# Encoder step: the last quarter of gate a moved from plain gate products into seven-product units; loads, output rows and the last product in another order

## The chip, the cores and the metric

The kernel runs on one core of a Trainium2 chip, in one launch. The metric is the device time of the whole program in microseconds (us). TensorE (PE) multiplies, VectorE (DVE) and ScalarE (ACT) do elementwise work, GpSimd (POOL) a little of it; SyncE (SP), POOL and ACT issue DMAs.

## The reference

One inference step of a one-layer encoder over 1024 prompt rows and 64 sample rows, 1088 in all, model width 1024:

```python
proj = rmsnorm(x, g_mix) @ w_in                     # 1024 -> 5120
cb, cc, ch, q, k, v, ga, gb = split(proj)           # six of 512, then ga and gb of 1024
ya = (cb * conv3(cc * ch)) @ w_conv_out             # 512 -> 1024, causal, width 3
yb = band_attention(q, k, v, rel_bias) @ w_attn_out # 8 heads of 64, own chunk of 64 and 8 before it
x  = x + (sigmoid(ga) * ya + sigmoid(gb) * yb) @ w_out
x  = x + (silu(n @ w_ff1) * (n @ w_ff3)) @ w_ff2    # n = rmsnorm(x, g_ffn)
y  = rmsnorm(x, g_final)
```

Outputs are also the last conv rows and the newest keys and values. All is float32.

## The kernel before

*Precision.* Each operand is split into a rounded high part and a low part (`split`, L128 on ACT and L129 on DVE), and a product is three matmuls: high by high, high by low, low by high. Activations lie transposed, with 1088 tokens in two halves of 544 columns (HT), each made of two pieces of 272 (HN).

*Units of seven.* A projection of 256 output channels can run as a unit (`run`, L277): the 2x2 blocks of weights and of tokens are combined so that seven block products do the work of eight (`STEPS`), each of 4 blocks x 3 x 2 pieces. The sums of the operands lie in `xn` and `xs`. q, k, cc, ch, cb and three quarters of gate a (`ga` 0 to 2) are such units, then four units `ya` of half the depth, whose operands `uforms` writes over those of the projections during the last unit before them. Results of ga get a sigmoid and go to `ga_d` in DRAM; `gated_load` fetches them, `ya_done` multiplies (the last quarter of ya is stored without its gate), and the rows go to `y_d`. One quarter of `xn`, which ya overwrites in part, is kept in `x21_d` and reloaded on SP before the gates.

*Gates and attention.* The other gate channels are plain products (`gate`, L343 to L345), with eight matmuls where a unit has seven: the eight blocks of gate b, then blocks 6 and 7 of gate a. A gate has four pieces of 272 columns, 24 matmuls each. Attention is a generator of 75 steps, nine token tiles for each of eight heads: scores, softmax, transposition two steps later, product with the values three steps later. After each gate piece `between` runs PER = 3.15 steps, so gate matmuls fill the time in which PE would wait for a softmax. The first eight pieces have no steps: they cover the loads of head 0 (`head_load`). Before the last LAST = 2 gates the remaining steps are flushed; the two gates after that cover the way of the head rows: `combine` stores them in `o_d`, they are loaded into `ob`, scaled by the softmax sums (L1160) and split. The last two gates write their sigmoids to SBUF (`ga_rows`).

*Output rows.* For each of eight blocks m, `yb` (L343 to L345 again, on `ob`) is multiplied by sigmoid(gb) (L1187), added to the row of y (L1188) and split into `mg`; the 64 sample columns are split once more into `ms`. For m of 6 and 7 the row of y is first multiplied by `ga_rows` (L1179). `rows_in` loads the rows four blocks ahead. Then come the product with w_out in two halves of columns (`wo_half`, loaded on SP), the feed-forward units (tiles `Aa` to `Db`), and the down product (L1750), whose last tiles pass the final norm (`half_ended`) to the output.

*Order.* The Tile scheduler orders each engine's instructions when it builds the program: by the order of the program text and by its own estimate of when operands are ready, so that a later instruction can be put ahead of one that it expects to wait. `tc.issue_after(i)` adds an edge behind instruction i on the same engine. On the chip each engine then runs its list in order.

Of the kernel before, what the change touches and what calls it, by code (L numbers as in the profile page):

```python
# [66 lines left out]
def encoder_kernel(ctx: ExitStack, tc: tile.TileContext, ins, outs):  # L67
# [268 lines left out]
    def product(out, w, x, o, n):  # L336

        kt = 4 * len(w)
        for k in range(kt):
            a, b = (t[:, k % 4] for t in w[k // 4])  # L340
            p, q = x.at(0, k, o, n), x.at(1, k, o, n)
            first, then = (q, p) if x is xn and o // HN % 2 == 0 else (p, q)
            mm(out, a, first, start=k == 0, stop=False)  # L343
            mm(out, a, then, start=False, stop=False)  # L344
            mm(out, b, p, start=False, stop=k == kt - 1)  # L345

    PIECES = [(j * HN, HN) for j in range(4)]
    GATES = [("b", m) for m in range(8)] + [("a", m) for m in range(6, 8)]
    for g, m in GATES:
# [3 lines left out]
        plan.append((ld, KD, m % 2 * P))  # L353
    for m in range(0, 8, 2):
        ld = {"src": ins["w_attn_out"][0][:, m * P : (m + 2) * P], "w": 2 * P, "at": 40}
        plan += [(ld, 4, j * P) for j in range(2)]
# [353 lines left out]
    def ya_done(u):  # L710
        def f(r, h, src, snap):
            if u == 3:
                s = summed(src, snap, "ya")
            else:
                g = gated.pop((u, r, h))
                if snap is None:
                    s = snap1(None, "ya")
                    two = [t.rearrange("p (j n) -> p j n", j=2) for t in (s, g)]
                    vec.tensor_tensor(two[0], src, two[1], op=ALU.mult)
                else:  # L720
                    s = summed(src, snap)
                    vec.tensor_tensor(s, s, g, op=ALU.mult)
            nc.gpsimd.dma_start(row_of(y_d, u, r, h), s)

        return f
# [110 lines left out]
    for n in range(len(units)):  # L836
        if n in (5, 6):
            for j in range(2):
                table_store(2 * (n - 5) + j)
        if n in (4, 5):  # L840
            for j in range(2):
                table_load(2 * (n - 4) + j, slot(STAGE, 768))
        if n == 0:
            r, si = r0, 2
        else:
            if n + 1 < len(units):
                nxt_unit = unit_of(n + 1)
                new = [(nxt_unit, {1: (), 2: (0, 1, 2)} if n == 1 else {})]
            else:
                new = [(PlainNext(), {})]  # L850
            if n == 1:
                ahead += new
                r, si = r1, 2
            else:
                r, si = run1(n, unit, new), 0
            unit = nxt_unit
        if n >= 12 and n < 15:
            gated_load(n - 12)
        if n == 14:
            plain_load(0)  # L860
        for _ in r:
            if n == 12:
                uforms(si)
            if n < 2 and si in (2 + n, 5 + n):
                i = 2 * n + si // 5
                cache_tile(i)
                if i + 2 < 4:
                    cache_load(i + 2)
            if si > 1:
                for f in due:  # L870
                    f()
                due.clear()
            due += late
            late.clear()
            si += 1
# [37 lines left out]
    sm2 = at_pool.tile([P, 2, 9], F32, name="sm2", bufs=1)  # L913
    nc.gpsimd.memset(sm2, 1.0)

    def head_load(h):
# [9 lines left out]
        for l in range(2):  # L926
# [7 lines left out]
        nc.sync.dma_start(v.bitcast(F32), v_d[h, :TP].rearrange("(b p) e -> p b e", p=P))  # L934
# [3 lines left out]
        b = bb[:, h % 2]  # L938
        near = bias_d[h, 127 : 127 + P * 383].rearrange("(p n) -> p n", n=383)
        far = bias_rows(h, 0, 384)  # L940
        nc.sync.dma_start(b[:HD, :384], far[:HD])
        nc.sync.dma_start(b[HD:, HD:384], far[HD:, HD:])
        nc.sync.dma_start(b[:HD, 384:576], near[:HD, :192])
        nc.sync.dma_start(b[HD:, 384:], near[HD:, :256])
        heads[h] = (q, k, ks, v, vs, b)

# [176 lines left out]
    def rows_in(m):  # L1123
        t, z = rows[m] = u_rows.tile([P, T], F32, tag="yg", name=f"yg{m}"), row_tile((m % 5 + 1) % 2, f"gb{m}")
        nc.sync.dma_start(z, gb_d[m * P : (m + 1) * P])
# [3 lines left out]

    for l in range(2):  # L1130
        nc.sync.dma_start(xn.t[0, 1][:, :, l].bitcast(F32), x21_d[:, l])
    for i in range(4):
# [8 lines left out]
    for i in range(4, len(GATES)):  # L1141
        gate_w[i] = next_w()
        if i == len(GATES) - LAST:
# [7 lines left out]
            u_rows = pg_stack.enter_context(tc.tile_pool(name="u_rows", bufs=5, reuse_waits="tile"))  # L1151
            ga_rows = [uo.tile([P, T], F32, name=f"ga{m}") for m in (6, 7)]
            for k in range(2):
                split(ob.t[:, 0, k], ob.t[:, 1, k], o_rows[k])
            late_r = row_tile(1, "rc2"), row_tile(0, "rc3")
            for k, r in zip((2, 3), late_r):
# [4 lines left out]
                split(ob.t[:, 0, k], ob.t[:, 1, k], r)  # L1161
            for m in range(4):
                rows_in(m)
# [8 lines left out]
    for m in range(8):  # L1172
        wb = next_w()
        if m + 4 < 8:
            rows_in(m + 4)
        t, z = rows.pop(m)
        act.activation(z, z, AF.Sigmoid)
        if m >= 6:
            vec.tensor_tensor(t, t, ga_rows[m - 6], op=ALU.mult)  # L1179
# [27 lines left out]
    def wo_half(hf):  # L1207
        r = []
        for kq in range(2):
            raw = rpool.tile([P, 4, 512], F32, tag="raw", name=f"wor{hf}_{kq}")  # L1210
            nc.sync.dma_start(
                raw,
# [471 lines left out]

    def half_ended(i, d):


        x = acc[i, d]
        ssq = dp.tile([P, 1], F32, tag=f"ssq{d}", name=f"ssq{i}_{d}", bufs=2)
        act.activation(ring_of(1)[:, 3072:3584], x, AF.Square, accum_out=ssq)  # L1690
        if i not in parts:
# [12 lines left out]
    for b, ks in enumerate(blocks):  # L1704
        first, final = b == 0, b == len(blocks) - 1
        nk = blocks[b + 1] if not final else []
        for g in range(2):
# [28 lines left out]
            for si, js in turns:  # L1736
                p, ht = STEPS[si], hts[base + si]
                key = {1: "A", 6: "A", 5: "A", 3: "A", 2: "B", 7: "D", 4: "D"}[p]
                for j in js:
# [6 lines left out]
                    t = ps[key, j]  # L1746
                    for k, kp in enumerate(ks):
                        w = W2[kp].w[p]
                        for n, (x, l) in enumerate(((0, 0), (0, 1), (1, 0))):
                            mm(  # L1750
                                t, ht[k][:, j, x], w[:, l],
                                start=p in (1, 2, 7) and k == 0 and n == 0,
                                stop=k == len(ks) - 1 and n == 2, skip_group_check=p in (6, 5, 4, 3),
                            )
# [4 lines left out]
                    if first and fresh:  # L1759
                        sums_at[0] = act.copy(o, t).ins  # L1760
# [7 lines left out]
                    if final and p in (5, 4, 3):  # L1768
                        half_ended(i + 4 * h, d)
                if js[-1] == 0:  # L1770
# [66 lines left out]
```

## Time and profile before

| what | us |
|---|---|
| median of 3 runs (1464.16 to 1465.11) | 1465.03 |
| the profiled execution | 1465.99 |
| its span, first to last instruction | 1464.2 |
| PE busy in the span | 1447.3 |
| DVE busy | 996.1 |
| ACT busy | 681.6 |
| POOL busy | 144.5 |

Matmuls overlap in the pipeline, so that the sum of their durations says little; a stretch divided by its count of matmuls gives the pace. A wait in square brackets is the idle time of the engine before an instruction, with what ended it. Names are those of the program's tiles.

### The profile page before, as it was taken

What the parts mean: (1) busy time and instruction counts of PE and PEld (TensorE: products, weight loads), DVE (VectorE), ACT (ScalarE), POOL (GpSimd) and SP (SyncE); (2) the same over time, 40 slices, a digit from 0 to 9 for tenths busy, and PEclk for the clock granted to TensorE, in tenths of its full rate; (3) what the DMA queues carried; (4) which work ended last, traced back from release to release, by engine and by line L of the source; (5) the groups of instructions that cost most, each with busy time, mean ns of one, the idle gap of its engine ahead of it and who ended that gap; (6) DMA issues with size and microseconds to landing.
All of it is one profiled execution on the core that took longest, in us unless ns stands there. A gap on an engine that the chain in (4) does not pass through costs nothing.

```text
span 1464.2 us, 26244 instructions
## 1 busy us (share of the span) xinstructions
PE 1447.3 (99%) x10128; PEld 1359.8 (93%) x10128; DVE 996.1 (68%) x1845; ACT 681.6 (47%) x1368; POOL 144.5 (10%) x262
## 2 busy tenths in 40 slices
PE   8999999999999999999999999999999999999997
PEld 6899999999999989998889999999999999888886
DVE  7975475658357677583588667766666668857676
ACT  7654343336357666541455444444344445512223
POOL 1400010001211121000100111111011111000000
PEclk9999999999999999999999999999999999999999
DMA  8686522234787675834432444443334448877685
GB/s 287 183 277 224 177 75 72 67 111 167 254 233 210 175 196 140 290 122 135 158 109 78 162 160 158 151 168 126 123 132 169 148 180 312 281 229 250 208 269 202
DMA packets 157212, 262.47 MB, mean 179 GB/s; under 512 B 18496, under 2 KB 89344, under 8 KB 157088
## 3 DMA queue, kind: packets, MB, share of 16 engines
q1 hardware_dynamic: 134416, 188.53, 40.7%
q0 software_dynamic: 21520, 70.19, 13.4%
q8 instruction: 79, 1.29, 0.4%
q10 hardware_dynamic: 1152, 2.10, 0.4%
q14 instruction: 45, 0.37, 0.1%
HBM read 171.78 MB, written 90.81 MB: 179 GB/s over the span
## 4 chain that ended last, share of the span: by engine, by line
PE 75%; issue 14%; DVE 5%; DMA 3%; ACT 2%; POOL 1%; SPq 0%; POOLq 0%; ACTq 0%; DVEq 0%
PE Ab L277 9%; PE Aa L277 8%; PE A L1750 8%; PE Db L277 4%; PE Da L277 4%; PE D L1750 4%; PE B L1750 2%; PE Bb L277 2%; PE Ba L277 2%; PE wo L1229 2%; PE wo L1231 2%; PE wo L1230 2%; PE t L1040 2%; PE Ak L277 2%; PE Aq L277 2%
## 5 line engine op out<-in xcount | busy, mean ns | idle before, releaser
L343 PE MATMUL g<-xn,wp 128*128 128x272 f32 x320 | 94.0, 294 | 0.0
L344 PE MATMUL g<-xn,wp 128*128 128x272 f32 x320 | 93.2, 291 | 0.0
L345 PE MATMUL g<-xn,low 128*128 128x272 f32 x320 | 92.9, 290 | 0.0
L128 ACT CAST ring<-w2r 128x512 fp32r<-128x512 f32 (+1 forms) x78 | 42.8, 587 | 94.9 <-PE A L1750 50.2
L951 DVE CUSTOM_DVE_ANT_0 p<-s,bb 128x640 f32<-128x640 f32 (+5 forms) x72 | 47.6, 663 | 39.8 <-DMA gb_d<-gst 27.2
L1750 PE MATMUL A<-ring,low 128*128 128x512 f32 x264 | 72.4, 389 | 0.0
L1750 PE MATMUL A<-ring,ht 128*128 128x512 f32 x264 | 72.3, 390 | 0.0
L129 DVE TENSOR_TENSOR low<-rawa,wa 128x512 fp32r<-128x512 f32 x55 | 37.7, 687 | 42.0 <-ACT wa L128 42.0
L343 PEld LDWEIGHTS g<-xn,wp 128*128 128x128 f32 x320 | 60.3, 189 | 0.6
L344 PEld LDWEIGHTS g<-xn,wp 128*128 128x128 f32 x320 | 60.3, 188 | 0.6
L345 PEld LDWEIGHTS g<-xn,low 128*128 128x128 f32 x320 | 60.2, 188 | 0.4
L1750 PEld LDWEIGHTS A<-ring,low 128*128 128x128 f32 x264 | 49.6, 188 | 10.3
L1750 PEld LDWEIGHTS A<-ring,ht 128*128 128x128 f32 x264 | 49.3, 188 | 10.5 <-ACT acc L1760 0.4
L129 DVE TENSOR_TENSOR ring<-w2r,ring 128x512 fp32r<-128x512 f32 (+1 forms) x78 | 48.9, 647 | 14.3 <-ACT ring L128 14.1
L277 PE MATMUL Ab<-tt,wb 128*128 128x272 f32 x352 | 57.8, 285 | 0.4 <-ACT wb L128 0.4
L277 PE MATMUL Ab<-mg,wb 128*128 128x272 f32 x352 | 58.0, 286 | 0.0
L277 PE MATMUL Aa<-mg,wa 128*128 128x272 f32 x352 | 57.7, 285 | 0.0
L277 PE MATMUL Aa<-tt,wa 128*128 128x272 f32 x352 | 57.7, 285 | 0.0
L961 ACT ACTIVATE p<-p,mx 128x640 f32<-128x640 f32 (+5 forms) x72 | 50.8, 706 | 13.5 <-DVE mx L951 13.2
L128 ACT CAST wa<-rawa 128x512 fp32r<-128x512 f32 x55 | 34.0, 621 | 47.1 <-PE Ab L277 33.3
L129 DVE TENSOR_TENSOR pt<-t,pt 128x640 fp32r<-128x640 f32 (+2 forms) x64 | 41.8, 653 | 15.5 <-ACT pt L128 14.7
L128 ACT CAST wb<-rawb 128x512 fp32r<-128x512 f32 x55 | 34.0, 621 | 38.3 <-PE Aa L277 24.5
(583 smaller groups left out, 4504.0 us busy)
## 6 DMA issues: line engine op xcount, KB each, us to landing
h_d<-hq POOLq DMA_DIRECT2D x44, 512.0 KB, 4.2
ht<-h_d SPq DMA_DIRECT2D x77, 256.0 KB, 3.5
low<-h_d SPq DMA_DIRECT2D x77, 256.0 KB, 3.8
h_d<-hq_early POOLq DMA_DIRECT2D x29, 512.0 KB, 4.0
rawa<-in_w_ff SPq DMA_DIRECT2D x11, 1024.0 KB, 5.7
rawb<-in_w_ff SPq DMA_DIRECT2D x11, 1024.0 KB, 5.4
w2r<-in_w_ff SPq DMA_DIRECT2D x11, 1024.0 KB, 7.3
qd<-q_d SPq DMA_DIRECT2D x32, 272.0 KB, 4.1
```

Source lines behind the costliest of these rows:

```text
L128: a = act.copy(hi, src)
L129: b = vec.tensor_tensor(lo, src, hi.bitcast(F32), op=ALU.subtract)
L277: newest[0] = mm(t[:, j, :HN], w[:, k, :], x[p][:, k, l, j * HN : (j + 1) * HN], start=p in (1, 2, 7) and k == 0 and n == 0, stop=k == las ...
L343: mm(out, a, first, start=k == 0, stop=False)
L344: mm(out, a, then, start=False, stop=False)
L345: mm(out, b, p, start=False, stop=k == kt - 1)
L951: vec.tensor_tensor_reduce(out=s if len(ps.shape) == 2 else s.rearrange("p (a b) -> p a b", a=2), in0=ps, in1=bias if len(ps.shape) == 2 e ...
L961: act.activation(s, s, AF.Exp, bias=mx, scale=-1.0, accum_out=sm)
L1040: nc.tensor.transpose(tp[:, i * P : (i + 1) * P], s[:, i * P : (i + 1) * P], ident)
L1229: mm(ps, x(k, 0), wh, start=f, stop=False)
L1230: mm(ps, x(k, 1), wh, start=False, stop=False)
L1750: mm(t, ht[k][:, j, x], w[:, l], start=p in (1, 2, 7) and k == 0 and n == 0, stop=k == len(ks) - 1 and n == 2, skip_group_check=p in (6, 5 ...
```

## The change

- Gate a's last quarter becomes a unit `ga` 3 in front of the ya units. `GATES` keeps the eight blocks of b; LAST is 1, PER is 3.8. `uforms` and the gate loads move on by one unit, and all four quarters of ya are multiplied by their gate in `ya_done`. `ga_rows` and its products disappear.
- The reload of `x21_d` is cut in two: blocks 2 and 3 during the first ya unit, 0 and 1 at the old place.
- For head 0 the four bias loads are issued ahead of the three value loads.
- The first block's yb products are ordered behind the last gate's last matmul.
- The sample columns are split by two POOL operations for each m, instead of two each on ACT and DVE.
- w_out is loaded by POOL's queue instead of SP's.
- The very last down product runs as two halves of 256 columns, with its addition and sum of squares in halves too.

```diff
-PER = 3.15
-LAST = 2
+PER = 3.8
+LAST = 1
...
-    GATES = [("b", m) for m in range(8)] + [("a", m) for m in range(6, 8)]
+    GATES = [("b", m) for m in range(8)]
...
-        ("ga", 1), ("cb", 1), ("ga", 2),
+        ("ga", 1), ("cb", 1), ("ga", 2), ("ga", 3),
...
     def ya_done(u):
         def f(r, h, src, snap):
-            if u == 3:
-                s = summed(src, snap, "ya")
-            else:
-                g = gated.pop((u, r, h))
...
+            g = gated.pop((u, r, h))
...
+    def x21_load(k):
+        for l in range(2):
+            nc.sync.dma_start(xn.t[0, 1][:, k : k + 2, l].bitcast(F32), x21_d[:, l, k : k + 2])
...
-        if n >= 12 and n < 15:
-            gated_load(n - 12)
+        if 13 <= n < 17:
+            gated_load(n - 13)
         if n == 14:
+            x21_load(2)
+        if n == 15:
             plain_load(0)
         for _ in r:
-            if n == 12:
+            if n == 13:
                 uforms(si)
...
-            if i >= len(GATES) - LAST:
-                act.activation(ga_rows[m - 6][:, o : o + n], ps[:, :n], AF.Sigmoid)
-                continue
...
+        if not h:
+            bias_load(h)
         v = hd_pool.tile([P, 8, P], F32R, tag="v", name=f"vd{h}")
...
+        if h:
+            bias_load(h)
...
-    for l in range(2):
-        nc.sync.dma_start(xn.t[0, 1][:, :, l].bitcast(F32), x21_d[:, l])
+    x21_load(0)
...
+    gates_end = newest[0]
...
-        if m >= 6:
-            vec.tensor_tensor(t, t, ga_rows[m - 6], op=ALU.mult)
+        late = t.rearrange("p (h n) -> p h n", h=2)[:, :, 512:]
+        hi, lo = (ms[:, m, l].rearrange("p (h n) -> p h n", h=2) for l in range(2))
...
-                product(yb[:, j, :HN], wb, ob, h * HT + j * HN, HN)
+                if n == 0:
+                    with tc.issue_after(gates_end):
+                        product(yb[:, j, :HN], wb, ob, h * HT + j * HN, HN)
+                else:
+                    product(yb[:, j, :HN], wb, ob, h * HT + j * HN, HN)
...
-            split(ms[:, m, 0, 32 * h : 32 * h + 32], ms[:, m, 1, 32 * h : 32 * h + 32], th[:, 512:])
+        pool_e.tensor_copy(hi, late)
+        pool_e.tensor_tensor(lo, late, hi.bitcast(F32), op=ALU.subtract)
...
-            nc.sync.dma_start(
+            nc.gpsimd.dma_start(
                 raw,
...
-    def half_ended(i, d):
+    def half_ended(i, d, ends=False):
...
+        if ends:
+            act.activation(ring_of(1)[:, 3072:3328], x[:, :256], AF.Square, accum_out=ssq)
+            vec.tensor_scalar(parts[i], ssq, 1.0 / D, parts[i], op0=ALU.mult, op1=ALU.add)
+            ssq = dp.tile([P, 1], F32, tag="ssq_e", name=f"ssq{i}_e")
+            act.activation(ring_of(1)[:, 3328:3584], x[:, 256:], AF.Square, accum_out=ssq)
...
+                    ends = final and g == 1 and js == (1,) and si == len(STEPS) - 1
+                    for c in ((slice(0, 256), slice(256, 512)) if ends else (slice(0, 512),)):
...
+                    if ends:
+                        for c in (slice(0, 256), slice(256, 512)):
+                            vec.tensor_tensor(o[:, c], t[:, c], o[:, c], op=ALU.add)
```

More of the change, by code (lines that the diff above doesn't have):

```diff
@@ L344, in product @@
             mm(out, a, then, start=False, stop=False)
-            mm(out, b, p, start=False, stop=k == kt - 1)
+            newest[0] = mm(out, b, p, start=False, stop=k == kt - 1).ins
     PIECES = [(j * HN, HN) for j in range(4)]
-    GATES = [("b", m) for m in range(8)] + [("a", m) for m in range(6, 8)]
+    GATES = [("b", m) for m in range(8)]
     for g, m in GATES:
@@ L353, in encoder_kernel @@
         plan.append((ld, KD, m % 2 * P))
-    for m in range(0, 8, 2):
+    MERGE = list(range(8))
+    for m in MERGE[::2]:
         ld = {"src": ins["w_attn_out"][0][:, m * P : (m + 2) * P], "w": 2 * P, "at": 40}
@@ L711, in f @@
         def f(r, h, src, snap):
[L712 to L722 removed]
+            g = gated.pop((u, r, h))
+            if snap is None:
+                s = snap1(None, "ya")
+                two = [t.rearrange("p (j n) -> p j n", j=2) for t in (s, g)]
+                vec.tensor_tensor(two[0], src, two[1], op=ALU.mult)
+            else:
+                s = summed(src, snap)
+                vec.tensor_tensor(s, s, g, op=ALU.mult)
             nc.gpsimd.dma_start(row_of(y_d, u, r, h), s)
@@ L914, in encoder_kernel, with bias_load @@
     nc.gpsimd.memset(sm2, 1.0)
+    def bias_load(h):
+        b = bb[:, h % 2]
+        near = bias_d[h, 127 : 127 + P * 383].rearrange("(p n) -> p n", n=383)
+        far = bias_rows(h, 0, 384)
+        nc.sync.dma_start(b[:HD, :384], far[:HD])
+        nc.sync.dma_start(b[HD:, HD:384], far[HD:, HD:])
+        nc.sync.dma_start(b[:HD, 384:576], near[:HD, :192])
+        nc.sync.dma_start(b[HD:, 384:], near[HD:, :256])
     def head_load(h):
@@ L1161, in encoder_kernel @@
                 split(ob.t[:, 0, k], ob.t[:, 1, k], r)
-            for m in range(4):
+            for m in MERGE[:4]:
                 rows_in(m)
@@ L1746, in encoder_kernel @@
                     t = ps[key, j]
[L1747 to L1754, printed above, removed]
+                    ends = final and g == 1 and js == (1,) and si == len(STEPS) - 1
+                    for c in ((slice(0, 256), slice(256, 512)) if ends else (slice(0, 512),)):
+                        for k, kp in enumerate(ks):
+                            w = W2[kp].w[p]
+                            for n, (x, l) in enumerate(((0, 0), (0, 1), (1, 0))):
+                                mm(
+                                    t[:, c], ht[k][:, j, x], w[:, l, c],
+                                    start=p in (1, 2, 7) and k == 0 and n == 0,
+                                    stop=k == len(ks) - 1 and n == 2, skip_group_check=p in (6, 5, 4, 3),
+                                )
                     h, d, fresh = {
@@ L1758, in encoder_kernel @@
                     o = acc[i + 4 * h, d]
-                    if first and fresh:
+                    if ends:
+                        for c in (slice(0, 256), slice(256, 512)):
+                            vec.tensor_tensor(o[:, c], t[:, c], o[:, c], op=ALU.add)
+                    elif first and fresh:
                         sums_at[0] = act.copy(o, t).ins
@@ L1768, in encoder_kernel @@
                     if final and p in (5, 4, 3):
-                        half_ended(i + 4 * h, d)
+                        half_ended(i + 4 * h, d, ends)
                 if js[-1] == 0:
```

21 lines of the change are left out of this document (7 added, 14 removed).

## The prediction

> **What bounds the kernel now.** I read the page first: the busy shares, then the chain that ended last.
>
> ```profile
> span 1464.2 us, 26244 instructions
> PE 1447.3 (99%) x10128; PEld 1359.8 (93%) x10128; DVE 996.1 (68%) x1845; ACT 681.6 (47%) x1368; POOL 144.5 (10%) x262
> PE 75%; issue 14%; DVE 5%; DMA 3%; ACT 2%; POOL 1%; SPq 0%; POOLq 0%; ACTq 0%; DVEq 0%
> ```
>
> TensorE (PE) is busy for 99% of the span, and the chain is mostly PE. One matmul's duration overlaps the next one's, so the price of a matmul is a stretch divided by its matmuls. The busy times of chosen stretches give that (stretch, length, then busy time and count of each engine, granted clock, DMA share, GB/s):
>
> ```profile
> core 0: us, PE busy (x) PEld busy (x) DVE busy (x) ACT busy (x) POOL busy (x), PEclk, DMA share, GB/s
> 302.00:323.00 21.00, 21.00 (x173) 21.00 (x172) 10.86 (x21) 7.38 (x14) 0.00 (x0) 1.00 0.22 80
> 373.50:384.70 11.20, 11.20 (x92) 11.15 (x91) 8.56 (x14) 5.88 (x10) 2.91 (x6) 1.00 0.87 270
> 384.00:410.00 26.00, 26.00 (x211) 26.00 (x210) 1.48 (x3) 4.22 (x10) 5.86 (x15) 1.00 0.91 284
> 411.70:592.40 180.70, 178.04 (x1274) 163.88 (x1272) 129.85 (x327) 127.39 (x314) 32.77 (x60) 1.00 0.69 190
> 613.70:663.00 49.30, 48.27 (x385) 47.99 (x384) 38.87 (x69) 20.73 (x44) 0.00 (x0) 1.00 0.45 149
> 1456.20:1464.20 8.00, 0.00 (x0) 0.00 (x0) 3.42 (x11) 2.46 (x6) 0.00 (x0) 0.76 0.37 139
> ```
>
> In 384 to 410, gates alone, 211 matmuls of 272 columns take 26.0 us: 0.123 us each, without a gap. In 302 to 323, a unit of seven products, the pace is the same. So the kernel is a queue of matmuls; a change pays by removing matmuls or by closing the few places where that queue stands still. Where the gates lie:
>
> ```profile
> 384.70:411.70 27.00, 26.95 (x216) 26.94 (x216) 3.09 (x8) 1.00 0.90 276
> 411.70:592.40 180.70, 91.75 (x578) 78.13 (x576) 9.25 (x24) 1.00 0.69 190
> 592.40:613.80 21.40, 21.30 (x168) 21.06 (x168) 2.73 (x7) 1.00 0.87 294
> ```
>
> These are gate matmuls alone: 216 before the first score, 576 inside attention as its filler, 168 after its last product.
>
> **The change, part by part.**
>
> *Work.* Two gates go: 2 x 4 pieces x 8 blocks x 3 = 192 matmuls, 23.6 us. One unit ga3 comes: 7 products x 4 blocks x 3 x 2 = 168, 20.7 us. That is 24 fewer: **-2.9 us**. Bounds: none worth naming, since both paces are rows. The unit's casts, sums and four sigmoids run beside its matmuls as in 302 to 323, where VectorE (DVE) has 10.9 and ScalarE (ACT) 7.4 us of 21. Its four stores and four loads of the gate rows, and its 1 MB of weights, are new on SP; DMA share there is 0.22. The last quarter of ya now multiplies by the gate: four DVE products of 544 columns, each half of the 1088-column product shown further down (1.29), 2.6 us, against 2.6 us idle in 373.5 to 384.7. DVE is then full there, and late work would be the last PSUM reads before the gates: 0 taken, +0.5 at worst.
>
> *Attention's start.* Half of the x21 reload moves on SP to the first ya unit, and head 0's four bias loads pass its three value loads.
>
> ```profile
> 384.69 1.23 SPq L1131 DMA_DIRECT2D xn<-x_d  x2
> 405.04 0.53 SPq L934 DMA_DIRECT2D vd<-v_d  x1
> 408.72 0.59 SPq L944 DMA_DIRECT2D bb<-bias_d  x1
> 413.23 0.29 DVE L951 CUSTOM_DVE_ANT_0 p<-s,bb 128x128 f32<-128x128 f32 x1 [27.19 <-DMA gb_d<-gst]
> 413.59 0.45 PE L993 MATMUL s<-kd,qd 128*128 128x384 f32 x1 [1.02 <-DVE mx L951]
> ```
>
> The first softmax starts 4.5 us after the last bias load is issued, and PE stands 1.02 us for it (the DMA that the profile names is a store that had nothing to do with it). Bias loads three issues (some 1.8 us) earlier, behind a queue with 1.1 MB less in it (4 us at 284 GB/s), are ahead of that: **-1.0 us** (0 to -1.0). Next late would be the values, which the third step needs some 6 us after the first score; they are put back by four issues, 2.5 us, and gain the same 4.
>
> *Attention itself.* Filler falls from 24 pieces to 20, 480 matmuls, for the same 75 steps, 3.8 steps a piece instead of 3.15 (20 x 3.8 = 76, enough). The stretch shrinks from 180.7 to about 169 us, so DVE's 129.9 us and ACT's 127.4 become 77% and 75%: neither binds. PE's idle there is 180.70 - 178.04 = 2.66 us, 1.02 of it counted above. The other 1.64 may vanish (-1.6) or, with less to slip in between, triple (+3.3). A sixth less filler; I take a third more idle: **+0.5**.
>
> *After attention.* Here cover goes. Only one gate instead of two stands between the last product and the output product yb, which needs the head rows written, read back, scaled and split.
>
> ```profile
> 591.60 0.89 PE L1052 MATMUL pv<-pts,vsd 128*128 128x128 f32 x5
> 592.93 0.19 ACT L967 COPY ca_s<-pv 64x64 f32<-64x64 f32 x1
> 593.65 1.09 SPq L976 DMA_DIRECT2D o_d<-co_s  x2
> 594.91 3.43 SPq L1158 DMA_DIRECT2D ob<-o_d  x2
> 598.51 0.41 PE L343 MATMUL yb<-ob,wp 128*128 128x272 f32 x2
> 599.92 1.29 DVE L1160 TENSOR_TENSOR rc<-ob,rc 128x1088 f32<-128x1088 f32 x1 [3.27 <-DMA ob<-o_d]
> 603.57 1.29 DVE L1160 TENSOR_TENSOR rc<-ob,rc 128x1088 f32<-128x1088 f32 x1 [1.76 <-DMA ob<-o_d]
> 604.90 1.10 ACT L128 CAST ob<-rc 128x1088 fp32r<-128x1088 f32 x1 [1.75 <-DVE rc L1160]
> 606.58 1.29 DVE L129 TENSOR_TENSOR ob<-rc,ob 128x1088 fp32r<-128x1088 f32 x1
> ```
>
> The last quarter of ob is whole at 607.9, 15.4 us after PE's last product at 592.5; now 168 gate matmuls hide that. 24 of the 192 of those gates ran ahead, inside attention's end. Afterwards 96 - 24 = 72 remain: 9.0 us. Then PE has yb matmuls whose ob is ready: three quarters of four groups, 36, 4.4 us. 15.4 - 9.0 - 4.4 = 2.0 us of standing. If PE's order takes one group to its end first, 9 matmuls (1.1 us) precede the wait: 5.3 us. If the chain is quicker with less beside it, nothing. I take **+2.0** (0 to 5.3), because the row at 598.51 shows two first-block matmuls of yb put ahead of 120 gate matmuls: the order does mix groups. The new ordering edge only keeps yb from blocking the last gate.
>
> *Output rows.* In 613.7 to 663, 382 yb matmuls need 47.1 of 49.3 us: 2.2 lost.
>
> ```profile
> 642.13 1.29 DVE L1179 TENSOR_TENSOR yg<-yg,ga 128x1088 f32<-128x1088 f32 x1 [0.42 <-DMA yg<-y_d]
> 644.85 0.39 PE L343 MATMUL yb<-ob,wp 128*128 128x272 f32 x1 [1.03 <-DVE gb L1187]
> L128 ACT CAST ms<-yg x16: 210/213/218, 618.9 to 666.3; 128x32 fp32r<-128x32 f32 x16
> L129 DVE TENSOR_TENSOR ms<-yg,ms x16: 183/184/189, 619.7 to 667.0; 128x32 fp32r<-128x32 f32 x16
> ```
>
> The two products by gate a (2 x 1.29), which wait at DVE's head for a row that nobody else needs yet, disappear; so do 16 x 0.18 us of sample splits, moved to GpSimd (POOL). PE's 1.03 us wait goes, and I give it half of the other 1.2: **-1.6** (0 to -2.2). POOL has no work in this stretch, and the sample rows are first used behind four tiles of the next product; a row buffer is freed a little later, and five of them rotate.
>
> *Loads of w_out* change queue, SP to POOL.
>
> ```profile
> L128 ACT CAST low<-wor x16: 602/621/622, 626.1 to 710.6; 128x512 fp32r<-128x512 f32 x16
> L129 DVE TENSOR_TENSOR wo<-wor,low x16: 680/685/693, 627.1 to 711.8; 128x512 fp32r<-128x512 f32 x16
> L1211 SPq DMA_DIRECT2D wor<-in_w_out x4: 383/384/384, 612.0 to 666.3; - x4
> DMA to landing us min/median/max: 5.0/6.6/7.9
> 673.47 0.55 POOL L1269 DMA_DIRECT2D x_d<-xr  x1 [70.26 <-DVE xr L1247]
> 712.21 0.54 POOL L1269 DMA_DIRECT2D x_d<-xr  x1 [5.35 <-DVE xr L1247]
> ```
>
> All four go out by 666.3, ahead of POOL's first waiting store at 673.5: 0. What they now stand behind is POOL's copies (rival below). SP, freed, issues its row loads earlier: 0.
>
> *Tail.* The last product runs as two halves of 256 columns.
>
> ```profile
> 1456.32 0.68 DVE L1762 TENSOR_TENSOR acc<-A,acc 128x512 f32<-128x512 f32 x1
> 1457.09 0.63 ACT L1690 ACTIVATE ring<-acc 128x512 fp32r<-128x512 f32 x1 [0.46 <-DVE n2y L185]
> 1458.22 0.21 DVE L183 TENSOR_SCALAR n0y<-ssq,more 128x1 f32<-128x1 f32 x1
> ```
>
> Addition and square behind the last matmul shrink by half of 0.68 and 0.63, 0.6 us; but the square waited on DVE's order, and nine more matmuls and three small operations join: **-0.3** (-0.6 to +0.2).
>
> Sum: -2.9 - 1.0 + 0.5 + 2.0 - 1.6 - 0.3 = **-3.3 us**. The profiled execution took 1465.99 us and would take 1462.7; it lies 1.0 above the median of the runs, 1465.03, from which I get **1461.7**.
>
> **A rule weighed.** In the last 8.0 us, with PE idle, the granted clock averages 0.76; every earlier stretch above has 1.00. The Trainium skill ("TensorE: Matmul & The Clock Gate", Part 1: The HAM clock gate) says that PE falls to half speed after an idle window of about 3.4 us and needs as long to come back. The trace agrees with the fall: 0.24 x 8.0 = 1.9 us lost is half speed for 3.8 us, from 4.2 us of idleness on. It shows no return. By the page's window, an estimate, a hole of 5.3 us would cost 1.7 us more; one of 2.0 nothing.
>
> **Rivals.**
>
> 1. *The hole isn't filled* (PE finishes one yb group first). 5.3 instead of 2.0: 1465.0, no change. For it: the row at 598.51 holds two such matmuls, not six. Against: they are of two groups. If the clock also falls, for as long as the last row shows it (1.9 us): 1466.9.
> 2. *Attention pays for the thinner filler*: +3.3 instead of +0.5, 1464.5. For it: softmax and split alternate on ACT and DVE at 70%. Against: only 1.64 us idle now.
> 3. *It doesn't do what it says*: bias still lands late and yb still stands 2.2 us: 1464.3.
> 4. *Slower: POOL's order.* If the first w_out loads stand behind POOL's copies of a late row, which waits for that row's product, they start too late. The first product starts at 663.0, a load took up to 7.9 us and a split 0.6 + 0.7: it decides from an issue after 653.8. Behind the copy of the row before last, some 661, PE stands 7 us: 1469. For it: POOL runs strictly in order, as its 70 us wait shows. Against: on SP the first load went out at 612.0, when no copy is due yet.
>
> **How the numbers follow.** My forecast 0.60, rival 1 0.14 (clock included in 0.04 of it), rival 2 0.10, rival 3 0.06, rival 4 0.10. A measurement tells about 0.2%, 2.9 us, from no change: faster means under 1462.1. My forecast lies barely there, but its open ends reach further down than up: 0.50 of its 0.60 is faster, 0.10 same. Same: 0.10 + 0.14 + 0.10 + 0.06 = 0.40. Slower: 0.10. Low end: hole 0, attention -1.6, rows -2.2: 1461.7 - 2.0 - 2.1 - 0.6 = 1457.0. High end: rival 1 with the clock, 1467.0; rival 4 is left out. The forecast's own range is 1457.0 to 1463.
>
> **What would show it.** 10128 - 24 + 9 = 10113 matmuls. A unit ga3 at 0.123 us a matmul. No wait of a third score for the first softmax. From attention's last product to yb: about 9 us of gates, 36 mixed yb matmuls, then a wait of about 2 us; 5 us and a clock under 1.00 mean rival 1. Idle in attention under 2.5 us; 5 means rival 2. No wait of yb for L1187. w_out issued on POOL before 654. The forecast fails if any of these stretches is off by more than 2 us.

## The result and the profile after

The changed kernel takes 1474.4 us (median of six runs, 1472.3 to 1476.1) beside 1464.8 for the kernel before on the same chip: ratio 1.0064, 95% interval 1.0054 to 1.0074. It is slower by 9.6 us, where 3.3 us faster was forecast, and lies above the range. The profiled execution took 1474.22 us.

The page of the changed kernel:

```profile
span 1472.4 us, 26272 instructions
PE 1449.7 (98%) x10113; PEld 1360.8 (92%) x10113; DVE 997.6 (68%) x1843; ACT 683.2 (46%) x1356; POOL 154.3 (10%) x281
```

The span is 8.2 us longer with 15 matmuls fewer, as many as foretold. So the work went as planned and the queue of matmuls now stands still somewhere. The busy times of chosen stretches of the changed kernel, in the columns of before:

```profile
core 0: us, PE busy (x) PEld busy (x) DVE busy (x) ACT busy (x) POOL busy (x), PEclk, DMA share, GB/s
432.30:604.90 172.60, 171.57 (x1218) 157.50 (x1216) 126.26 (x325) 124.69 (x310) 31.50 (x58) 1.00 0.70 186
604.90:609.20 4.30, 4.28 (x33) 4.06 (x33) 1.81 (x4) 1.32 (x4) 1.36 (x2) 1.00 0.40 102
609.20:621.60 12.40, 4.09 (x15) 3.23 (x15) 7.15 (x7) 5.04 (x7) 1.30 (x2) 0.60 0.97 360
621.60:628.00 6.40, 6.40 (x38) 6.40 (x39) 2.63 (x4) 1.69 (x2) 0.00 (x0) 0.71 1.03 418
628.00:669.60 41.60, 41.60 (x335) 41.60 (x334) 32.43 (x48) 18.86 (x27) 6.94 (x15) 1.00 0.40 138
```

The first row is attention, from the first score to the last product with the values; it is as dense as before. Then 33 gate matmuls, and then a hole: 53 matmuls in 18.8 us, where 0.123 us each would be 6.5. 12.3 us are lost there. After 628 nothing stands. The gate matmuls alone, in the three stretches that were shown of before (216, 576 and 168 there):

```profile
405.30:432.30 27.00, 26.97 (x216) 26.92 (x216) 3.10 (x8) 1.00 0.96 290
432.30:604.90 172.60, 85.85 (x522) 71.54 (x520) 8.35 (x22) 1.00 0.70 186
604.90:609.20 4.30, 4.28 (x33) 4.06 (x33) 0.39 (x1) 1.00 0.40 102
```

Gates begin at 405.3 instead of 384.7, 20.6 us later: the unit ga3, as priced. Inside attention stand about 519 gate matmuls, and only 33 are left behind it. The prediction had 480 and 72. PE's waits in the last stretch, and the chain that they wait for, in order of time (the sign <- names what ended the wait):

```profile
PE yb L343 <- ACT ob L128: 5.5, 2, 3.7
PE yb L344 <- DVE ob L129: 2.8, 2, 2.0
```

```profile
598.39 1.11 ACT L1182 ACTIVATE gb<-gb 128x1088 f32<-128x1088 f32 x1 [0.73 <-DMA gb<-gb_d]
599.53 0.69 ACT L128 CAST pt<-t 128x640 fp32r<-128x640 f32 x1
600.25 0.82 DVE L129 TENSOR_TENSOR pt<-t,pt 128x640 fp32r<-128x640 f32 x1 [2.66 <-ACT pt L128]
...
603.99 0.89 PE L1059 MATMUL pv<-pts,vsd 128*128 128x128 f32 x5
...
607.60 0.78 POOL L1221 DMA_DIRECT2D wor<-in_w_out  x1
608.12 2.92 SPq L1163 DMA_DIRECT2D ob<-o_d  x2
609.89 2.10 ACT L128 CAST ob<-o 128x1088 fp32r<-128x1088 f32 x2
611.05 0.51 PE L343 MATMUL yb<-ob,wp 128*128 128x272 f32 x2 [1.87 <-ACT ob L128]
611.12 0.76 POOL L1221 DMA_DIRECT2D wor<-in_w_out  x1
612.77 0.43 PE L345 MATMUL yb<-ob,low 128*128 128x272 f32 x1
616.20 1.29 DVE L1165 TENSOR_TENSOR rc<-ob,rc 128x1088 f32<-128x1088 f32 x1 [2.68 <-DMA ob<-o_d]
618.68 0.82 PE L343 MATMUL yb<-ob,wp 128*128 128x272 f32 x2 [3.67 <-ACT ob L128]
618.93 1.29 DVE L1165 TENSOR_TENSOR rc<-ob,rc 128x1088 f32<-128x1088 f32 x1 [1.44 <-DMA ob<-o_d]
620.14 2.54 DVE L129 TENSOR_TENSOR ob<-rc,ob 128x1088 fp32r<-128x1088 f32 x2
621.48 0.59 PE L344 MATMUL yb<-ob,wp 128*128 128x272 f32 x1 [1.98 <-DVE ob L129]
```

Four things can be read here. A sigmoid of a gate row stands on ACT ahead of attention's last large cast, waits for its load, and DVE and PE stand behind it; PE fills that with gate matmuls, which are then missing later. The w_out loads, now on POOL, go out beside the loads of `ob`, and these come in only at 616.2 and 618.9, 8.1 us after their issue instead of 5. ACT casts the two early quarters of `ob` only at 609.9. And ob is whole at 622.7, 17.8 us after the last product with the values (15.4 before), with 4.1 us of gates in front of it.

PE's waits sum to 8.3 us; the other 4.0 of the 12.3 lost are the clock. 53 matmuls were busy 4.09 + 6.40 = 10.5 us instead of 6.5, and one took 0.43 us instead of 0.29. The mean clock of 0.60 over 12.4 us and 0.71 over 6.4 us makes 13.6 us at half speed, if the clock is counted as either full or half.

### The profile page after: what moved, and what is told of

It reads as the page before. It is cut to its first block, busy times and chain, and to the rows that moved or that the text cites. A ratio compares the mean times of both kernels' runs of the same rounds, so it can differ in the third digit from the quotient of the medians.

```text
span 1472.4 us, 26272 instructions
## 1 busy us (share of the span) xinstructions
PE 1449.7 (98%) x10113; PEld 1360.8 (92%) x10113; DVE 997.6 (68%) x1843; ACT 683.2 (46%) x1356; POOL 154.3 (10%) x281
## 5 line engine op out<-in xcount | busy, mean ns | idle before, releaser
L344 PE MATMUL g<-xn,wp 128*128 128x272 f32 x256 | 75.3, 294 | 0.0
L343 PE MATMUL g<-xn,wp 128*128 128x272 f32 x256 | 75.0, 293 | 0.0
L345 PE MATMUL g<-xn,low 128*128 128x272 f32 x256 | 74.8, 292 | 0.0
L1767 PE MATMUL A<-ring,ht 128*128 128x512 f32 (+1 forms) x267 | 72.7, 388 | 0.7 <-ACT acc L1780 0.7
L1767 PE MATMUL A<-ring,low 128*128 128x512 f32 (+1 forms) x270 | 72.6, 384 | 0.0
L968 ACT ACTIVATE p<-p,mx 128x640 f32<-128x640 f32 (+5 forms) x72 | 50.9, 707 | 12.7 <-DVE mx L958 12.4
L1239 PE MATMUL wo<-low,mg 128*128 128x512 f32 x128 | 50.9, 397 | 0.0
L1241 PE MATMUL wo<-wo,mg 128*128 128x512 f32 x128 | 50.1, 391 | 0.0
L1240 PE MATMUL wo<-low,mg 128*128 128x512 f32 x128 | 49.9, 390 | 0.0
```

Source lines behind the costliest of these rows:

```text
L345: newest[0] = mm(out, b, p, start=False, stop=k == kt - 1).ins
L968: act.activation(s, s, AF.Exp, bias=mx, scale=-1.0, accum_out=sm)
L1239: mm(ps, x(k, 0), wh, start=f, stop=False)
L1240: mm(ps, x(k, 1), wh, start=False, stop=False)
L1241: mm(ps, x(k, 0), wl, start=False, stop=e)
L1767: mm(t[:, c], ht[k][:, j, x], w[:, l, c], start=p in (1, 2, 7) and k == 0 and n == 0, stop=k == len(ks) - 1 and n == 2, skip_group_check=p ...
```

## The experiments

Theories: T1, ACT's early sigmoid stalls the end of attention, and the stall eats the cover. T2, the w_out loads on POOL collide with the loads of ob. T3, too few gate matmuls are left as cover. T4, ACT casts ob too late. Each kernel's time stands beside the kernel before, run on the same chip beside it; "over before" is the difference of the two medians. For the changed kernel it is 9.6 us. With four runs of a kernel the interval is about 2 us either way.

### e1: w_out back on SP

```diff
 def wo_half(hf):
-            nc.gpsimd.dma_start(
+            nc.sync.dma_start(
```

> The changed kernel with its w_out loads put back on SP's queue, behind the head rows and the gate rows (nothing else is edited). In the changed kernel the two last head-row loads of ob took 8.06 and 8.19 us from issue to landing, beside w_out loads issued at 607.60 and 611.12, and ob was whole 17.8 us after the last pv. Theory T2 (the w_out loads on POOL's queue take bandwidth from the row loads): the two loads come back to 5 to 6 us, ob is whole about 15 us after the last pv, and the time falls by 2.5 to 4 us, to 1470.4 to 1471.9. Theories T1 (ACT's early sigmoid eats the gates that should cover the hole), T3 (one gate is too little cover whatever the loads do) and T4 (ACT's order of casts): no change beyond 1 us, 1473.4 to 1475.4. If the loads of blocks behind it suffer instead, up to 1 us slower.

Measured: 1474.2, 8.1 over before (ratio 1.0055, 1.0040 to 1.0070). SP's queue and the landing of ob's loads in this kernel:

```profile
608.98 0.53 SPq L1221 DMA_DIRECT2D wor<-in_w_out  x1
609.67 2.36 SPq L1163 DMA_DIRECT2D ob<-o_d  x2
```

```profile
DMA to landing us min/median/max: 8.2/8.5/8.9
```

The scheduler put the first w_out load ahead of ob's, and they took 8.2 to 8.9 us again. So POOL as the issuing queue isn't to blame, and the collision itself was not removed. T2 stayed open.

### e2: the sigmoids late

```diff
-        act.activation(z, z, AF.Sigmoid)
+        if n < 4:
+            with tc.issue_after(att_end):   # attention's last copy on ACT
+                act.activation(z, z, AF.Sigmoid)
+        else: ...
```

> The changed kernel with the sigmoids of the first four gate rows issued on ACT behind attention's last pv copy, so that none stands ahead of attention's last casts. T1: the 3.3 us stall at attention's tail is gone, the last pv ends about 1.7 us sooner, and 47 gate matmuls are left behind it instead of 33; the chain of the rows begins sooner by the same 1.7 us, so the time falls by 1.5 to 3 us, to 1471.4 to 1472.9 (the rest of the hole stays, since the work in it is the same). T2, T3, T4: the sum of work and waits is set by the row chain alone; within 1 us of 1474.4. Against T1: the sigmoid now runs in the hole and holds ACT 2.4 us (table load and sigmoid) ahead of the casts of ob, which would take the gain back.

Measured: 1473.9, 7.8 over before (1.0055, 1.0038 to 1.0072). In the trace attention, from its first score to the end of its last product, takes 170.3 instead of 172.6 us, and the space behind it, up to the first product with w_out, grew from 64.7 to 66.7 us. T1 names a real stall, but taking it away only moves its time into the hole: 47 gate matmuls stand there instead of 33, and PE still waits 7.2 us for ob instead of 8.3. The sigmoid now stands ahead of the casts of ob, as the objection in the expectation said; that this is what takes the gain back isn't shown.

### e3: the casts of ob first

```diff
-                split(ob.t[:, 0, k], ob.t[:, 1, k], o_rows[k])
+                ob_cast = split(ob.t[:, 0, k], ob.t[:, 1, k], o_rows[k])[0]
...
+            if i == len(GATES) - 1 and c > 1:
+                with tc.issue_after(ob_cast): act.copy(st[:, :n], ps[:, :n])
```

> The changed kernel with the copies of the last gate's third and fourth unit issued on ACT behind the casts of ob's first two quarters. T4 (the casts came at 609.89 to 612.0 though their data were there, behind weight splits and those copies): they come about 1 us sooner, PE's first wait in the hole (2.03 us) shrinks by 1 us and the time falls by 0.5 to 1.5 us, to 1472.9 to 1473.9. T1, T2, T3: the last quarter's chain decides, no change, 1474.0 to 1474.8. If the copies now hold the last gate's banks, up to 0.5 us slower.

Measured: 1472.6, 6.5 over before (1.0048, 1.0030 to 1.0066). Better than either theory said, but the interval reaches the changed kernel's. PE still waited 8.4 us for ob.

### e4: two gates kept behind

```diff
-PER = 3.8
-LAST = 1
+PER = 4.7
+LAST = 2
```

> The changed kernel with LAST = 2 and PER = 4.7 instead of 1 and 3.8: attention is dealt over six gates and two gates are kept to stand behind it, with all else as in the changed kernel. T3 (cover): about 70 gate matmuls stand behind the last pv instead of 33, 4.6 us more work in the hole; idle time there falls from 13 us to 6 or less, the clock is not halved, and the time falls by 5 to 9 us, to 1465.4 to 1469.4. T1 and T4: as much, since the hole is covered in either case. T2: the row loads stay at 8 us, ob is whole 17 to 18 us after the last pv, and only 3 to 5 us come back, 1469.4 to 1471.4. If attention lacks filler with six gates, idle time inside it grows from about 4 us, and the gain is given back there: 1472 or more.

Measured: 1469.0, 2.9 over before (1.0021, 1.0012 to 1.0030; ten runs, 1466.3 to 1470.9): 6.7 us of the 9.6 are gone. Its profile is that of its fastest run. The stretches as above, and PE's waits in them:

```profile
432.30:599.70 167.40, 167.23 (x1181) 153.19 (x1179) 125.68 (x325) 123.18 (x308) 30.40 (x56) 1.00 0.72 190
599.70:608.50 8.80, 8.80 (x71) 8.80 (x71) 3.62 (x5) 4.45 (x8) 1.67 (x3) 1.00 0.69 179
608.50:620.00 11.50, 8.60 (x46) 7.95 (x45) 7.55 (x9) 5.06 (x6) 2.07 (x3) 0.73 1.00 384
```

```profile
PE yb L344 <- DVE ob L129: 2.5, 2, 1.7
PE yb L343 <- ACT ob L128: 0.4, 1, 0.4
```

The same eight gates, dealt otherwise: attention needs 37 gate matmuls fewer, is 5.2 us shorter without standing, and 70 are left. This agrees with T3: how the cover is dealt decides how much is left. The hole is still there: 2.9 us of waits, none over 1.7 us, and again a halved clock (0.27 x 11.5 / 0.5 = 6.2 us at half speed). Not all of the gain need be cover. The landing of ob's two loads in this kernel:

```profile
DMA to landing us min/median/max: 4.9/5.0/5.1
```

They were issued from 602.6 on, and the first w_out load, still on POOL, followed only at 610.5: with the shorter attention the collision of T2 is gone as well. How the 6.7 us divide between the two isn't shown; e6 below prices the loads.

### e6: w_out behind the rows

```diff
+            rows_first = newest[2]          # the first four blocks' last row load
...
+            with tc.issue_after(rows_first):
+                nc.sync.dma_start(raw, ...)
```

> The changed kernel with its w_out loads on SP's queue and placed there behind the first four blocks' gate and y rows (when they were only put back on SP they went ahead of ob's loads, and the row loads still took 8.88 and 8.19 us, so the collision had not been taken away). Now no w_out load runs before ob is whole. T2 (collision): ob's two loads fall from 8.1 to 5 or 6 us, ob is whole 2.5 to 3 us sooner, time 1470.5 to 1472. T3 (the chain behind the last pv is too long for 33 gate matmuls whatever its loads do): the gate and y rows, issued right behind, fill the DMA engines instead, the loads stay over 7 us, and the time stays within 1 us of 1474.4. If the w_out loads, now behind rows that wait for buffers, come after 654, the first wo waits and the time rises instead.

Measured: 1472.2, 6.6 over before (1.0047, 1.0032 to 1.0062). The landing of ob's two loads:

```profile
DMA to landing us min/median/max: 5.1/5.2/5.2
```

T2's numbers, in the loads and, within 0.2 us, in the time: the loads are back to 5.2 us, and the first product with w_out did not come later. PE's waits for ob fell only from 8.3 to 6.3 us. The collision is real in the loads; by the medians it is worth some 2 to 3 us, at the edge of what four runs tell.

### e7: work added to the hole

```diff
             product(ps[:, :n], gate_w[i], xn, o, n)
+            if i == len(GATES) - 1 and c == 3:
+                for _ in range(2):
+                    with tc.issue_after(pv_end):   # the last product with the values
+                        product(ps[:, :n], gate_w[i], xn, o, n)
```

> The changed kernel with the last gate unit's product computed three times instead of once, the two extra ones (48 matmuls, 5.9 us at 123 ns) placed behind the last pv; the result is the same. PE has more work, none of it useful. If the lost time is waiting alone, the extra products go into the waits and the time stays at 1474.4 within 1 us (or rises by what does not fit). If the halved clock in the hole is a loss of its own (granted clock 0.60 over 12.4 us, then 0.71 over 6.4 us, matmuls at 227 ns), the extra products keep PE busy, the clock stays at 1.00 and 3 to 4.5 us come back: 1470 to 1471.5. More work making the kernel faster would show the clock's share.

Measured: 1471.8, 6.3 over before (1.0047, 1.0032 to 1.0062). 48 matmuls more, and the time did not rise; by the medians it fell by 3.3 us. The upper half of that, that the clock alone returns 3 us, isn't shown: the intervals overlap, and the profiled execution was its slowest run (1474.3), with the clock still at 0.72 in the last 12 us of the hole. Shown is that the useless work did not lengthen the program. It shifted other work, too: the first w_out load went out at 618.0 instead of 607.6, and ob's loads took 6.5 to 7.0 us instead of 8.1, so some of the time may have come back there.

### e10: the last gate held

```diff
-            product(ps[:, :n], gate_w[i], xn, o, n)
+            if i == len(GATES) - 1:
+                with tc.issue_after(pv_end):
+                    product(ps[:, :n], gate_w[i], xn, o, n)
+            else: ...
```

> The changed kernel with the whole last gate (96 matmuls, 11.9 us) placed behind the last pv, so that none of it can run ahead into attention's stalls; nothing else is edited. T3: cover in the hole rises from 4.1 to 11.9 us, the waits there shrink from 8.3 us to about 1 to 3 us and the clock is not halved, which is worth 10 us in the hole; attention loses 63 gate matmuls as filler (7.8 us), and if it still runs without idle time it is shorter by as much: 1464 to 1467. If attention needs those 63 as filler, its idle time grows from 1 us by up to 7 us, and the time is 1468 to 1472. T1 (the early sigmoid) gives attention a stall of about 3 us with nothing to fill it: 1467 to 1469.

Measured: 1474.0, 8.5 over before (1.0058, 1.0041 to 1.0075): no gain, and above every time that was forecast. Stretches and waits:

```profile
432.70:605.40 172.70, 165.27 (x1155) 150.26 (x1153) 126.36 (x325) 124.04 (x309) 30.40 (x56) 0.99 0.71 185
605.40:618.80 13.40, 13.40 (x97) 13.40 (x98) 7.86 (x9) 5.38 (x8) 2.04 (x4) 0.89 0.76 222
```

```profile
PE rt L1034 <- DVE pt L129: 3.7, 1, 3.7
PE yb L343 <- DVE gb L1201: 3.2, 2, 2.0
```

The hole is covered, and the first w_out load went out only at 618.4, so that ob's loads took 4.0 to 5.2 us. But attention without its 63 filling matmuls takes exactly as long, 172.7 us, with 7.4 us of idle time in it, 3.7 of them in T1's place. The same matmuls are missing, only in front of the last product instead of behind it.

### e11: the other parts of the change alone

Ten gates stand in attention as before (the diff's hunks on `GATES`, `units`, LAST, PER, `ya_done`, `ga_rows` taken back); everything else is as in the changed kernel.

> The other parts of the change alone: ten gates stand in attention as before (gate a's last quarter among them, LAST 2, PER 3.15, its two row products in the merge), with the changed loads of x21 and of the bias, the sample split on POOL, the w_out loads on POOL, the new order edge and the tail in halves. If the loss comes from moving two gates out of attention (cover and filler), it isn't here: attention's start gains 1.0 us, rows 0 to 1, so 1463 to 1465 where the kernel before takes 1465. If w_out on POOL's queue, or the new edge, is what breaks the stage behind attention, it is here too: 3 us or more slower than before, 1468 or above.

Measured: 1463.7, 1.4 **under** before (ratio 0.9988, 0.9978 to 0.9997; ten runs). Attention, the gates behind it, the output rows:

```profile
412.10:591.20 179.10, 177.88 (x1275) 163.97 (x1273) 129.72 (x327) 127.08 (x314) 32.86 (x60) 1.00 0.68 184
591.20:612.40 21.20, 21.20 (x171) 21.20 (x171) 10.18 (x12) 12.84 (x20) 1.59 (x2) 1.00 0.85 309
612.40:660.30 47.90, 47.90 (x385) 47.90 (x384) 37.36 (x54) 17.67 (x27) 7.67 (x16) 1.00 0.51 169
```

This settles where the loss is from: all of it comes with the move of the two gates out of attention. w_out on POOL, the new edge and POOL's splits cost nothing as long as 21 us of gates stand behind attention.

### e12: three small causes together

The edits of e2, e3 and e6 in one kernel.

> The changed kernel with three edits together that brought 0.5, 1.8 and 2.2 us alone: gate rows' sigmoids behind attention's last copy, casts of ob's first half ahead of the last gate's copies, w_out loads behind the first rows. If the three are separate losses, they add: 4 to 5 us, 1469.5 to 1470.5. If they are one chain, seen from three sides (whatever else is late sets ob's time), the sum is no more than the largest: 1471.5 to 1473. In neither case does it come under the kernel before, since cover is still some 47 matmuls, 5.8 us, for a chain of 15 us.

Measured: 1472.0, 6.9 over before (1.0047, 1.0032 to 1.0062). By the median no more than the largest of the three alone, which speaks for the second reading, one chain seen from three sides; the interval, 4.7 to 9.1 us over, doesn't quite exclude the lower end of the sum. The traces say the same: the first product with w_out comes at 667.4 here, 667.3 in e6, 668.6 in e3, 670.1 in e2 and 669.6 in the changed kernel.

### e13: gates cut

```diff
-            product(ps[:, :n], gate_w[i], xn, o, n)
+            product(ps[:, :n], gate_w[i][:1] if i > 5 else gate_w[i], xn, o, n)
```

> The changed kernel with its last two gates summed over half of their depth (their result is another): 96 gate matmuls less, 11.9 us of PE work, all from the end of attention and from behind it. If PE's work sets the time there, the kernel gets 9 to 12 us faster, 1462 to 1465. If attention and the head rows are chains of latency, and gate matmuls only fill their gaps, the work that goes turns into idle time: 0 to 3 us faster, 1471 to 1474, with idle time and half clock grown by 9 us or more; with the clock halved for longer, even slower.

Measured: 1474.4, 9.2 over before (1.0051, 1.0032 to 1.0071). 11.9 us of PE work were taken away, and by the median nothing came back (three runs at 1473.9 to 1474.8, one at 1469.0). Attention, and what follows it up to 628:

```profile
432.70:607.80 175.10, 167.06 (x1154) 151.33 (x1152) 127.95 (x328) 125.62 (x314) 34.21 (x62) 0.99 0.75 200
607.80:628.00 20.20, 10.84 (x46) 9.85 (x46) 9.41 (x10) 7.21 (x8) 0.00 (x0) 0.52 0.76 275
```

Attention is 2.5 us longer than in the changed kernel with 8.0 us of idle time, and then PE works 10.8 of 20.2 us, at half clock. This is the reading of latency chains in numbers: at eight gates, a gate matmul in this region has a price that these four runs can't tell from zero. The cut moved loads as well: the first w_out load went out at 594.1 instead of 607.6, and ob's last two loads were issued 4.6 us behind the last product with the values instead of 3.2, so part of what the cut brought may have been lost there.

### e14: an earlier start

The changed kernel with LAST = 2, PER = 4.42, e3's order of casts, and

```diff
         gate(i, (0, 1))
+        if i == 3:
+            between()
```

> A version that may beat both: the changed kernel with LAST = 2 and PER = 4.42, attention's first step dealt right behind the fourth gate's first half instead of behind its third unit, and the casts of ob's first half ahead of the last gate's copies. 89 gate matmuls are then placed behind the last pv (70 with LAST = 2 alone, which took 1469.0). If cover is what lacks, 19 more matmuls, 2.3 us, plus a clock that is not halved (half for some 3 us in the profile of that run) give 3 to 5 us: 1464 to 1466, and level with the kernel before or 1 us under it. If attention cannot start sooner because head 0's loads land at 427 to 431, or its own chain only takes longer, it stays at 1468 to 1469.

Measured: 1469.1, 4.0 over before (1.0026, 1.0016 to 1.0037). The first score came at 429.4 instead of 432.3, and yet the time is e4's. 89 matmuls of cover did not help: PE still waited 2.5 us for ob, and another delay came behind it; on ACT:

```profile
625.76 1.11 ACT L1188 ACTIVATE gb<-gb 128x1088 f32<-128x1088 f32 x1 [3.62 <-DMA gb<-gb_d]
```

A sigmoid at ACT's head waits 3.6 us for its gate row, DVE stands behind it, and PE then stands 2.0 us at 630.9 for a bank of yb that DVE frees. The gain of 3 to 5 us didn't come. (The expectation put e4's half clock at some 3 us; e4's rows give 6.2.)

### e15: e11 without the tail's halves

```diff
-                    ends = final and g == 1 and js == (1,) and si == len(STEPS) - 1
+                    ends = False
```

> The ten-gate kernel with the change's other parts (1463.7 us), and its last product undivided again, to price the tail. The prediction gave the halves -0.3 us; in the traces the last matmul's end to the program's end is 8.05 us without them and 8.03 and 8.04 with them, and the last stage before it is 232.2 us without and 232.6 to 233.7 with them. If the halves are a loss of 0.4 us or more, the last stage comes back to 232.2 and the kernel takes 1463.0 to 1463.4; if the stage's differences are chance, the trace shows 232.6 or more again and the time is 1463.7; if the halves gain, it is 1464.0. Whichever, it should be level with or 1 to 2 us under the kernel before.

Measured: 1463.5, 1.6 under before (0.9987, 0.9978 to 0.9996; eleven runs), the best version of all, though not told from e11. Its last stage and tail:

```profile
1221.30:1453.40 232.10, 232.10 (x1036) 192.26 (x1034) 166.31 (x297) 73.54 (x148) 3.21 (x6) 1.00 0.76 255
1453.40:1461.10 7.70, 0.01 (x1) 0.00 (x0) 3.43 (x11) 2.46 (x6) 0.00 (x0) 0.80 0.39 147
```

239.8 us together; in e11, with the halves, 241.2 (233.1 and 8.1). So the halves show no gain. Why the tail doesn't shrink is seen in the changed kernel:

```profile
1464.38 0.21 DVE L183 TENSOR_SCALAR n0y<-ssq,more 128x1 f32<-128x1 f32 x1 [0.79 <-ACT ring L1705]
1464.51 0.41 DVE L1778 TENSOR_TENSOR acc<-A,acc 128x256 f32<-128x256 f32 x1
1464.94 0.40 DVE L1778 TENSOR_TENSOR acc<-A,acc 128x256 f32<-128x256 f32 x1
1465.87 0.75 DVE L1715 SCALAR_TENSOR_TENSOR acc<-acc,n4y,gfb 128x512 f32<-128x512 f32 x1
1466.54 0.21 DVE L183 TENSOR_SCALAR n0y<-ssq_e,more 128x1 f32<-128x1 f32 x1
```

On DVE the first half's addition stands behind a small operation of the tile before, which waits for ACT; and the last tile's norm stands behind that tile's scaling. Shorter pieces do not pass what is ahead of them.

## Why the prediction was wrong

*Work*: right. 10113 matmuls, gates 20.6 us later. *Attention's start*: right; PE's wait of 1.02 us for the first softmax is gone, against -1.0. *Attention itself*: PE's idle time is 1.03 us in 172.6, below the forecast, so rival 2 fell, too. But the stretch is 172.6 us long and not 169: the scheduler put 39 more gate matmuls in it than the dealing by pieces had.

*After attention*: this is the step that failed, +2.0 us against about +12.3. Its working had four premises, and each went the same way. "24 of the 192 of those gates ran ahead" was taken as a constant: 63 of 96 ran ahead, and cover was 4.1 and not 9.0 us. Taking one stall away (e2) left 14 more behind, so stalls draw them in; with still fewer dealt to each step (e4), 122 of 192 ran ahead. What drew in the rest isn't shown. The chain of 15.4 us was taken from a stretch in which w_out's first load went out only at 612.0, behind it: beside w_out it was 17.8 (e6 shows the loads' share in it). "Three quarters" of ob were to be ready for mixing: PE waited for the first two already. And the clock was left out of the forecast, with 4.0 us. Rival 1 named the right place and sign, with a hole of 5.3 us and 1.9 of clock; it was some 5 us too small.

Behind the four lies, as I read the runs, one error. The removed 192 matmuls were priced at PE's pace, 23.6 us, because PE was busy for 99%. A busy PE there did not mean that PE sets the time: attention and the head rows are chains on ACT, DVE and DMA, and gate matmuls fill them. e13 and e7 give the marginal price, as far as four runs each and the loads that moved with them allow: 96 fewer bring nothing by the median, 48 more cost nothing. The right question was how many of the 744 behind the first score were surplus. Some 480 inside attention (e4; with 457 it stands for 7 to 8 us, e10 and e13) and 125 for a chain of 15.4 us make 605, less what yb can mix in. 552 were left, 53 too few, 6.5 us at PE's pace. The rest of the 12.3 us is how the 552 were dealt, the longer chain and the clock. This sum is an argument from the runs, not a run of its own, and no run splits the loss among them.

*Output rows*: right in kind. In e11, where nothing hides it, 385 matmuls take 47.9 us without a gap, and the row of before has 385 in 49.3: -1.4 of -1.6. *w_out*: priced at 0. Rival 4 did not occur (the first two loads went out at 607.6 and 611.1), but I had not asked what the two early loads collide with. *Tail*: -0.3 was forecast; e15's pair of traces has +1.4 for the halves, the medians +0.3, which they can't tell from nothing. The parts outside the gates sum to -1.4 us measured (e11), where -2.9 was forecast.

*The rule weighed*, that PE falls to half speed after an idle window of about 3.4 us (the Trainium skill, "TensorE: Matmul & The Clock Gate", Part 1: The HAM clock gate). The prediction read it as a bound on one gap, so that a hole of 2.0 us would cost nothing. The runs differ from that reading: in e4 no wait is over 1.7 us, and 6.2 us ran at half speed; in the changed kernel PE was dry from 609.2, with two matmuls at 611.1, and from 612.4 on they were slow. The return in the changed kernel agrees with the page: PE works without a gap from 621.5, and its matmuls are fast again at 625.3, 3.8 us later.

```profile
624.82 0.43 PE L343 MATMUL yb<-ob,wp 128*128 128x272 f32 x1
625.27 0.30 PE L345 MATMUL yb<-ob,low 128*128 128x272 f32 x1
```

Other runs spread around that: in e4 it took 6.1 us from the last wait (614.6 to 620.7), in e14 2.0 us (615.2 to 617.2, behind a wait of 0.48 us). What no run separates is how much of the loss would stay at full clock.

## What to carry to other kernels

Before work is taken out of a stretch in which one engine is busy, ask what that work covers: sum the latency chains beside it, and price only the surplus at the engine's pace. How many filler instructions an order leaves for the end is no constant; count them in the new order, since a scheduler spends them at the first stall. And loads moved to a freer queue start earlier: look at what they then run beside.

## What the runs showed of the hardware

A queue of matmuls broken by several short waits loses the clock as well: the changed kernel's hole, with waits of 1.9, 0.8, 3.7 and 2.0 us, spent 13.6 us at half clock, and e4's, with waits of at most 1.7 us, 6.2 us. With two 1 MB loads and the gate rows beside them, 0.5 MB row loads took 8.1 us from issue to landing instead of the 5.2 of e6, at 360 to 418 GB/s and all DMA engines busy. The queue that issued the 1 MB loads made no difference that shows: 8.2 to 8.9 us with SP (e1).
